# Two norms between mixer and channel mixer, taken by halves of the tokens

## The chip, the core and the metric

The kernel runs on one core of a Trainium2 chip. TensorE (PE) multiplies matrices into PSUM, VectorE (DVE) and ScalarE (ACT) do the elementwise work, GpSimd (POOL) a few small powers, and SyncE (SP) issues the DMAs. The metric is the device time of one execution in microseconds (us), lower is better.

## The reference

A hybrid layer (dilated attention and a linear recurrence) is followed by two layers of a second block. Only this block is touched. Each layer adds four token mixers, projected by `w_out`, to the residual stream `x` (512 tokens of 1024 channels), norms the sum, and adds a channel mixer:

```
x = x + mod_x[2] * token_mixers(...)          # concatenate([y_a, y_b, y_c, y_d]) @ w_out
x = x + mod_x[5] * channel_mixer(modulate(rms_norm_2(x, norm2_g[l]), mod_x[3], mod_x[4]), w1, w2)

rms_norm_2(x, g) = x * rsqrt(mean(x * x, axis=-1) + EPS) * g
modulate(h, shift, scale) = h * (1 + scale) + shift
channel_mixer(h, w1, w2) = square(relu(h @ w1)) @ w2      # 1024 -> 4096 -> 1024
```

In layer 0 a second stream of 256 context tokens goes through the same channel mixer. The norm needs the whole sum of a token's 1024 channels, so nothing of the channel mixer can start for a token before the last mixer's projection of that token is done.

## The kernel before

Activations lie transposed: 8 tiles of 128 channels by 512 tokens (context: 8 of 128 by 256). Every matrix product is made of three float32r matmuls (`mm3`, L157 to L159: high weights by high activations, high by low, low by high), so each operand is kept as a high part (ACT: `whi` L149, `h` L711) and a low part (DVE: `wlo` L150, `h` L712). Three buffers each hold the high and the low halves of a weight block (`W_BUFS = 3`), so a cast of new weights waits until PE has read the block three before.

The engines run their own queues in order; the order comes from a list scheduler with priorities. `tc.high_priority(offset=n)` moves instructions forward, and `bg(n)` (a negative offset) back.

At the place in question, once in each of the two layers, PE finishes the attention of the last mixer ("b"). `out_part("b")` then multiplies its result `y` by `w_out`: 8 output tiles of 128x512, 6 matmuls each. DVE adds every tile to the residual `x` (L1139), ACT squares it (L217), DVE adds the squares into `acc` (L221). Behind the last tile, `rstd_bcast` sums `acc` and the last square over channels on PE with one-column matmuls (L208, the squares are the weights, a column of ones moves), DVE scales (L233), POOL takes the power (L225), DVE spreads the result (L238), and PE transposes it into all partitions (L241). `modulate` then makes each of the 8 tiles of `h`: DVE multiplies (L709), ACT makes the high part (L711), DVE the low part (L712). The first pair of up-projection tiles (`up(0)`, called block 0 below; `up(1)` is block 1) goes through `gemm` with `together=True`, so that its tiles advance side by side. ACT takes the relu (L1283), DVE squares it (L1284) and splits the result into `hid`.

Of the kernel before, what the change touches and what calls it, by code (L numbers as in the profile page):

```python
# [10 lines left out]
F32 = mybir.dt.float32  # L11
# [8 lines left out]
P = 128  # L20
NT = 8
# [58 lines left out]
def tile_net(ctx: ExitStack, tc: tile.TileContext, wst, vec, crow, lrow, sgw, cst, xT, xN, cT, out):  # L80
# [117 lines left out]
    class Sums:  # L198


        def __init__(self, n, acc=None, bank=None):
            self.n, self.acc, self.bank, self.parts = n, acc, bank or (lambda: ps.mm()), [] if acc is None else [acc]

        def finish(self):
            pt, nt = self.bank(), self.n // P
            for k, a in enumerate(self.parts):
                for i in range(nt):
                    T.matmul(pt[:, i:i + 1], a[:, i * P:(i + 1) * P], ones1, start=k == 0 and i == 0,  # L208
                             stop=k == len(self.parts) - 1 and i == nt - 1, skip_group_check=True)
# [15 lines left out]
        G.tensor_tensor(rs[:, :n], ms, neghalf[:, :n], ALU.pow)  # L225
        return rs

    def rstd_bcast(pool, sums, n, inv, tile=None):
# [10 lines left out]
        pb = bank()  # L239
        for i in range(nt):  # L240
            T.transpose(pb[:, i * P:(i + 1) * P], rb[:, i], ident)  # L241
        return pb[:, :n]


    def silu_row(pool, tmp, name, idx):

        raw = pool.tile([P, 1024], F32, tag=name, name=name)
        nc.sync.dma_start(raw, crow[:, idx * 1024:(idx + 1) * 1024])
        for q in range(2):
            c = raw[:, q * 512:(q + 1) * 512]  # L250
            th = tmp("th")
            A.activation(th, c, AF.Tanh, scale=0.5)
            V.scalar_tensor_tensor(c, th, 1.0, c, op0=ALU.add, op1=ALU.mult)
        return raw
# [446 lines left out]
        else:  # L701
            affine1 = affine

    def modulate(pool, s, pb, off, acts, bufs=3):

        a_col, b_col = s.mod[:, off + 8:off + 16], s.mod[:, off:off + 8]
        for m in range(NT):
            t = pool.tile([P, s.n], F32, tag=f"r{s.name}", name=nm("mod"), bufs=bufs)
            V.scalar_tensor_tensor(t, s.x[m], a_col[:, m:m + 1], pb, op0=ALU.mult, op1=ALU.mult)  # L709
            a, b = acts[m], b_col[:, m:m + 1]  # L710
# [18 lines left out]
    def xsums():  # L729
        return Sums(SX, xp.tile([P, SX], F32, tag="acc", name=nm("acc")))  # L730
# [77 lines left out]
    class Mixer:  # L808
# [325 lines left out]
                    heads_norm(po, r1)  # L1134


        def add(self, m, p, done):
            s = self.s
            V.scalar_tensor_tensor(s.x[m], p, s.mod[:, 16 + m:17 + m], s.x[m], op0=ALU.mult, op1=ALU.add)  # L1139
            if done:  # L1140
                done(m)

        def out_part(self, names, done=None, bank=None):

# [44 lines left out]
    for l in range(2):  # L1189
# [60 lines left out]


        full = [sx, sc] if l == 0 else [sx]
        g_n, mlp = open_pool("mlp")
        sx.h = [mlp.tile([P, 2, SX], F32R, tag="hx", name=nm("h"), bufs=8) for _ in range(NT)]
        if l == 0:
            sc.h = [mlp.tile([P, 2, SC], F32R, tag="hc", name=nm("h"), bufs=8) for _ in range(NT)]
            g_c, cp = open_pool("cp", side="right")
            load_ctx(cp, lambda m: c_dram[m], cp)
            pbc = rstd_bcast(mlp, sc.acc, SC, 1.0 / 1024)
        modulate(mlp, sx, pbx, 24, sx.h)  # L1260
        if l == 0:
            modulate(mlp, sc, pbc, 24, sc.h)
            g_r, rowp = open_pool("rows1", side="right")
            rawa_bufs[0] = 1
            junk_fn[0] = lambda n: mlp.tile([P, SX], F32, tag="rx", name=nm(n), bufs=3)
            c2 = silu_row(rowp, junk_fn[0], "c2row", 1)
            cc = silu_row(rowp, junk_fn[0], "ccrow", 2)
            steps = ada_steps(1, lambda n="j": junk_fn[0](n))
        hid = {}
        nhid = [0]  # L1270

# [8 lines left out]
        def up(b):  # L1280
            def evac(s, i, p):
                r = mlp.tile([P, s.n], F32, tag=f"r{s.name}", name=nm("r"), bufs=3)
                A.activation(r, p, AF.Relu)  # L1283
                V.scalar_tensor_tensor(r, p, 0.0, r, op0=ALU.max, op1=ALU.mult)  # L1284
                a = hid_tile(s)
                split(a, r)
                hid[(s.name, 2 * b + i)] = a

            gemm(wblock((f"up{l}", b), 4, 256), 4, [(s, s.n, s.h) for s in full], evac, together=b == 0)

        def down(c, strs, last):
            if last:
# [11 lines left out]
                if l == 0:  # L1304
                    pump(1)

        for b in range(4):
            up(b)
        for c in range(4):
            if c < 3:  # L1310
                up(4 * c + 4)
                down(c, full, False)
                for b in range(4 * c + 5, 4 * c + 8):
                    up(b)
                    if l == 0:
                        pump(1)
            else:
                down(c, [sx], True)
                pbx = rstd_bcast(mlp, sx.acc, SX, 1.0 / 1024)
                if l == 0:  # L1320
                    pump(24)
                    for t, q in affine1:
                        ada_affine(t, vc("ada_b1"), q)
                    sx.mod = modx[1]
                    sx.h = [xact("h") for _ in range(NT)]
                    modulate(mlp, sx, pbx, 0, sx.h)
                    down(c, [sc], True)
                    close_pool(g_r)
# [32 lines left out]
VP = 7000  # L1361
HPS = 400
PT_BUFS = 2
PSA = dict(g=3, mm=2, po=1, big=1)
PSD = dict(g=3, mm=1, po=1, sc3=1)

# [138 lines left out]
```

## Time and profile before

| | |
|---|---|
| three timed runs, us | 2176.32, 2177.66, 2178.42 |
| median, us | 2177.66 |
| the profiled execution: its time, us | 2175.18 |
| the profiled execution: its span, first to last instruction, us | 2173.3 |
| mean granted TensorE clock | 0.978 |

The span lies inside the execution; 1.9 us of its time lie around it. [...]

### The profile page before, as it was taken

To read this page: it belongs to the slowest core of one execution; us is meant where nothing else is said; L and a number is where in the kernel's file an instruction comes from. 1 tells how busy PE (TensorE), PEld (TensorE's weight loads), DVE (VectorE), ACT (ScalarE), POOL (GpSimd) and SP (SyncE) were. 2 spreads that over 40 slices of the span, in tenths; PEclk is the share of its full clock that TensorE was granted. 3 is DMA by queue.
4 is the path that set the end of the run, shared out by engine and by line. 5 is a ranking of instruction groups with operands and counts; after the bars stand their busy time and mean duration, and the time that the engine had idled before them with its cause. 6 is when DMAs were issued, how large, how long until landed. Compare 5 with 4: busy or idle time off the path is not lost.

```text
span 2173.3 us, 28000 instructions
## 1 busy us (share of the span) xinstructions
PE 2053.4 (94%) x11020; PEld 1758.3 (81%) x11020; DVE 1424.4 (66%) x2351; ACT 810.1 (37%) x1266; POOL 27.4 (1%) x28
## 2 busy tenths in 40 slices
PE   7989999999999988998999999999998998999997
PEld 5778788778889777876888888888887787888886
DVE  8778999843458999778354645534798766443444
ACT  3565333432344533645312313123434544232331
POOL 0000000000000000000000000000000000000000
PEclk9999999999999999998999999999999998999998
DMA  8523666523335444222232454422413212333331
GB/s 314 171 92 95 197 222 204 181 94 105 109 111 168 124 121 127 78 78 79 67 127 88 138 169 150 155 67 89 135 59 107 83 59 69 97 97 97 97 97 58
DMA packets 84388, 259.47 MB, mean 119 GB/s; under 512 B 11424, under 2 KB 20256, under 8 KB 84256
## 3 DMA queue, kind: packets, MB, share of 16 engines
q1 hardware_dynamic: 84256, 257.67, 37.6%
q8 instruction: 87, 1.43, 0.3%
q14 instruction: 45, 0.37, 0.1%
HBM read 242.95 MB, written 5.24 MB: 114 GB/s over the span
## 4 chain that ended last, share of the span: by engine, by line
PE 72%; DVE 18%; DMA 3%; issue 3%; ACT 3%; POOL 1%; SPq 0%; POOLq 0%; DVEq 0%; ACTq 0%
PE mm L157 15%; PE mm L159 15%; PE mm L158 15%; PE g L157 5%; PE g L158 5%; PE g L159 5%; DVE wlo L150 3%; DVE ya L872 2%; PE po L1084 2%; DVE rawa L263 2%; DVE j L263 1%; PE sc L1057 1%; DMA rawa<-wst 1%; PE mm L1081 1%; PE mm L208 1%
## 5 line engine op out<-in xcount | busy, mean ns | idle before, releaser
L149 ACT CAST whi<-raw 128x1024 fp32r<-128x1024 f32 x312 | 326.9, 1050 | 536.7 <-PE mm L158 387.4
L150 DVE TENSOR_TENSOR wlo<-raw,whi 128x1024 fp32r<-128x1024 f32 x312 | 380.5, 1222 | 210.7 <-ACT whi L149 205.9
L157 PE MATMUL mm<-h,whi 128*128 128x512 f32 (+1 forms) x992 | 361.0, 366 | 5.7 <-ACT h L338 3.6
L158 PE MATMUL mm<-h,whi 128*128 128x512 f32 (+1 forms) x992 | 361.7, 365 | 0.9 <-DVE h L712 0.9
L159 PE MATMUL mm<-h,wlo 128*128 128x512 f32 (+1 forms) x992 | 361.1, 364 | 0.8 <-DVE wlo L150 0.8
L159 PE MATMUL mm<-hid,wlo 128*128 128x512 f32 (+1 forms) x768 | 272.6, 355 | 1.0 <-DVE wlo L150 1.0
L157 PE MATMUL mm<-hid,whi 128*128 128x512 f32 (+1 forms) x768 | 273.0, 355 | 0.0
L158 PE MATMUL mm<-hid,whi 128*128 128x512 f32 (+1 forms) x768 | 272.8, 355 | 0.0
L157 PEld LDWEIGHTS mm<-h,whi 128*128 128x128 f32 x992 | 188.8, 191 | 37.1 <-ACT h L338 4.0
L158 PEld LDWEIGHTS mm<-h,whi 128*128 128x128 f32 x992 | 188.7, 190 | 31.5 <-DVE h L712 1.9
L157 PE MATMUL g<-h,whi 128*128 128x512 f32 x512 | 205.7, 402 | 8.6 <-DVE v L508 6.0
L159 PEld LDWEIGHTS mm<-h,wlo 128*128 128x128 f32 x992 | 188.6, 190 | 31.2 <-DVE wlo L150 2.0
L158 PE MATMUL g<-h,whi 128*128 128x512 f32 x512 | 204.8, 400 | 0.0
L159 PE MATMUL g<-h,wlo 128*128 128x512 f32 x512 | 204.3, 399 | 0.3 <-DVE wlo L150 0.3
L159 PEld LDWEIGHTS mm<-hid,wlo 128*128 128x128 f32 x768 | 146.1, 190 | 21.5 <-DVE wlo L150 1.4
L157 PEld LDWEIGHTS mm<-hid,whi 128*128 128x128 f32 x768 | 146.4, 191 | 20.2
L158 PEld LDWEIGHTS mm<-hid,whi 128*128 128x128 f32 x768 | 146.3, 191 | 20.0
L1284 DVE SCALAR_TENSOR_TENSOR r<-mm,r 128x512 f32<-128x512 f32 x96 | 57.4, 599 | 114.1 <-ACT r L1283 114.0
L157 PEld LDWEIGHTS g<-h,whi 128*128 128x128 f32 x512 | 98.4, 192 | 26.9 <-issue 6.2
L159 PEld LDWEIGHTS g<-h,wlo 128*128 128x128 f32 x512 | 98.1, 192 | 19.3 <-DVE wlo L150 0.7
L158 PEld LDWEIGHTS g<-h,whi 128*128 128x128 f32 x512 | 98.3, 192 | 17.9
L872 DVE SCALAR_TENSOR_TENSOR ya<-glu,caw,ya 128x512 f32<-128x512 f32 (+1 forms) x180 | 111.6, 656 | 0.5
(309 smaller groups left out, 3462.7 us busy)
## 6 DMA issues: line engine op xcount, KB each, us to landing
raw<-wst SPq DMA_DIRECT2D x312, 512.0 KB, 3.9
rawa<-wst SPq DMA_DIRECT2D x120, 512.0 KB, 4.6
qst<-q SPq DMA_DIRECT2D x48, 64.0 KB, 2.0
kst<-k SPq DMA_DIRECT2D x48, 64.0 KB, 2.0
kst<-k SPq DMA_DIRECT2D x72, 32.0 KB, 2.1
x<-xT SPq DMA_DIRECT2D x4, 512.0 KB, 5.0
hs_d<-c SPq DMA_DIRECT2D x4, 512.0 KB, 2.6
hq<-hs_d SPq DMA_DIRECT2D x4, 512.0 KB, 5.5
```

Of the source, the lines that this page charges most:

```text
L149: A.copy(hi, src)
L150: V.tensor_sub(lo, src, hi.bitcast(F32))
L157: T.matmul(ps, lh, rh, start=start, stop=False)
L158: T.matmul(ps, lh, rl, start=False, stop=False)
L159: T.matmul(ps, ll, rh, start=False, stop=stop)
L208: T.matmul(pt[:, i:i + 1], a[:, i * P:(i + 1) * P], ones1, start=k == 0 and i == 0, stop=k == len(self.parts) - 1 and i == nt - 1, skip_gr ...
L263: V.tensor_tensor_reduce(o, w, row, 0.5, 0.0, ALU.mult, ALU.add, d)
L872: V.scalar_tensor_tensor(self.ya[m], x, w, self.ya[m], op0=ALU.mult, op1=ALU.add)
L1057: T.matmul(st[:, o:e], hd.q[:, w, qt * P:(qt + 1) * P], hd.k[:, w, o - w * nkeys:e - w * nkeys], start=True, stop=True, skip_group_check=True)
L1081: T.transpose(pt[:, i * P:(i + 1) * P], pw[0][:, t0 + i * P:t0 + (i + 1) * P], ident)
L1084: T.matmul(hd.po[:, qt, h % 2], pth[:, i * P:(i + 1) * P], ss.v[:, kt, h], start=i == 0 and qt == 0 and h % 2 == 0, stop=i == nk - 1 and q ...
L1284: V.scalar_tensor_tensor(r, p, 0.0, r, op0=ALU.max, op1=ALU.mult)
```

## The change

`out_tokens` replaces `out_part("b")`: it makes the 8 output tiles for tokens 0 to 255, then for tokens 256 to 511, in matmuls of 256 columns. The sums no longer go through `acc`: right behind each add, ACT squares the 128x256 half tile, and PE multiplies its two 128-token pieces by ones into a PSUM bank of the half (`Sums(now=...)`, `nb`), moved back by 10 or 60 in the scheduler's priority. Each half has its own `rstd_bcast`, its own `modulate` into its half of the tiles `h`, and its own pass of `up(0)`. `gemm` with `together=True` now goes over channels outside and tiles inside. In layer 0 the context's norm, modulation and first up-projection pair are written ahead of the first half's, at a priority raised by 150. PSUM is shared out as 6 banks and 2 for the halves, where it was 8.

```diff
             for h, (hi, lo) in enumerate(halves):
-                for (mi, (key, n, acts)), p in zip(grp, pss_):
-                    c = slice(mi * P, (mi + 1) * P)
-                    for k in range(kn):
+                for k in range(kn):
+                    for (mi, (key, n, acts)), p in zip(grp, pss_):
+                        c = slice(mi * P, (mi + 1) * P)
                         kk = h * kn + k
                         a = acts[kk]
                         mm3(p[:, :n], hi[:, k, c], lo[:, k, c], a[:, 0], a[:, 1], kk == 0, kk == kt - 1)
...
+        def product(self, pt, a, first, last):
+            for i in range(self.n // P):
+                T.matmul(pt[:, i:i + 1], a[:, i * P:(i + 1) * P], ones1, start=first and i == 0,
+                         stop=last and i == self.n // P - 1, skip_group_check=True)
...
             A.activation(sq, src, AF.Square)
-            if self.acc is None or m == NT - 1:
+            if self.now is not None:
+                with bg(self.back if m >= 6 else 10):
+                    self.product(self.now[:, SC:], sq, m == 0, m == NT - 1)
+            elif self.acc is None or m == NT - 1:
                 self.parts.append(sq)
...
+        def out_tokens(self, n, w, sl, done):
+
+            for m in range(NT):
+                p = ps.mm()[:, :SC]
+                hi, lo = w[m // 4]
+                c = slice(m % 4 * P, (m % 4 + 1) * P)
+                for kk in range(2):
+                    a = self.y[n, kk][:, :, sl]
+                    mm3(p, hi[:, kk, c], lo[:, kk, c], a[:, 0], a[:, 1], kk == 0, kk == 1)
+                self.add(m, p, done, sl)
...
-        ps = PS("ps_e", mm=8)
-        sx.acc = xsums()
-        mx.out_part("b", lambda m: sx.acc.add(None, sx.x[m], m, mx.tt("sq")))
-        pbx = rstd_bcast(mix, sx.acc, SX, 1.0 / 1024, tile=mx.tt("rb"))
+        ps = PS("ps_e", mm=6, nb=2)
+        g_n, nrm = open_pool("nrm", side="right")
+        wb = [whalf((f"out{l}", 2 + h), 1, 512) for h in range(2)]
+        pbs = []
+        for t in range(2):
+            acc, sl = Sums(SC, now=ps.mm("nb"), back=SUM_BACK[t]), TOK[t]
+            mx.out_tokens("b", wb, sl, lambda m: acc.add(
+                None, sx.x[m][:, sl], m, nrm.tile([P, SC], F32, tag="sq", name=nm("sq"), bufs=4)))
+            pbs.append(rstd_bcast(None, acc, SC, 1.0 / 1024, back=RB_BACK[t],
+                                  tile=nrm.tile([P, SC], F32, tag="rb", name=nm("rb"), bufs=2)))
+        close_pool(g_n)
...
+            with tc.high_priority(offset=CTX_HP):
+                load_ctx(cp, lambda m: c_dram[m], cp)
+                pbc = rstd_bcast(mlp, sc.acc, SC, 1.0 / 1024)
+                modulate(mlp, sc, pbc, 24, sc.h)
+        modulate(mlp, sx, pbs[0], 24, sx.h, sl=TOK[0])
+        up0 = wblock((f"up{l}", 0), 4, 256)
+        if l == 0:
+            up(0, up0, [sc])
+        up(0, up0, [sx], TOK[0])
+        modulate(mlp, sx, pbs[1], 24, sx.h, sl=TOK[1])
+        up(0, up0, [sx], TOK[1])
```

Three places show what this does to the engines' order, all in layer 0; layer 1 has the first two in the same form.

On PE, in the projection of the last mixer (`mm` are output tiles, `nb_8630` is the first half's bank of sums, `sq_8639` and `sq_8651` are squares of its first and second tile), before and then now:

```order
L157 MATMUL mm_8643<-y_8319,whi_8616 128x512
L158 MATMUL mm_8643<-y_8319,whi_8616 128x512
L159 MATMUL mm_8643<-y_8319,wlo_8617 128x512
L157 MATMUL mm_8643<-y_8606,whi_8616 128x512
L158 MATMUL mm_8643<-y_8606,whi_8616 128x512
L159 MATMUL mm_8643<-y_8606,wlo_8617 128x512
```

```order
L157 MATMUL mm_8655<-y_8606,whi_8618 128x256
L158 MATMUL mm_8655<-y_8606,whi_8618 128x256
L207 MATMUL nb_8630<-ones_66,sq_8639 128x1 x2
L159 MATMUL mm_8655<-y_8606,wlo_8619 128x256
L157 MATMUL mm_8667<-y_8319,whi_8618 128x256
L158 MATMUL mm_8667<-y_8319,whi_8618 128x256
L159 MATMUL mm_8667<-y_8319,wlo_8619 128x256
L207 MATMUL nb_8630<-ones_66,sq_8651 128x1
L157 MATMUL mm_8667<-y_8606,whi_8618 128x256
L207 MATMUL nb_8630<-ones_66,sq_8651 128x1
```

The sums of a half tile now stand among the projection's matmuls, the first of them 17 matmuls behind its start; of the 16 half tiles of a layer, 8 have their two columns together and 8 have a matmul in between, and those of the last three half tiles stand behind the projection.

On ACT, at the end of the projection (`whi_9030` and `whi_9229` are the weights of block 1's first half; their buffer is that of the second half of `w_out`), before and then now:

```order
L217 ACTIVATE sq_8690<-x_4800 128x512
L149 CAST whi_9030<-raw_9032 128x1024
L217 ACTIVATE sq_8701<-x_4801 128x512
L217 ACTIVATE sq_8712<-x_4802 128x512
L711 ACTIVATE h_8740<-mod_8811,der 128x512
```

```order
L223 ACTIVATE sq_8804<-x_4800 128x256
L149 CAST whi_9229<-raw_9231 128x1024
L223 ACTIVATE sq_8816<-x_4801 128x256
L223 ACTIVATE sq_8828<-x_4802 128x256
L723 ACTIVATE h_8855<-mod_8918,der 128x256
```

The cast that waits for PE's last read of `w_out` stays ahead of the last two squares.

On DVE, behind the last add of layer 0 (`nb_8735` is the second half's bank, `mm_8904` the context's sums, `h_8855` the context's first tile), now:

```order
L1152 SCALAR_TENSOR_TENSOR x_4802<-mm_8820,der,x_4802 128x256
L150 TENSOR_TENSOR wlo_9230<-raw_9231,whi_9229 128x1024
L242 TENSOR_SCALAR ms_8833<-nb_8735 128x2
L242 TENSOR_SCALAR ms_8909<-mm_8904 128x2
L247 COPY rb_8832<-rs_8835 128x256
L247 COPY rb_8913<-rs_8911 128x256
L721 SCALAR_TENSOR_TENSOR mod_8918<-xc_8867,der,mm_8915 128x256
L721 SCALAR_TENSOR_TENSOR mod_8922<-xc_8870,der,mm_8915 128x256
L721 SCALAR_TENSOR_TENSOR mod_8926<-xc_8875,der,mm_8915 128x256
L724 SCALAR_TENSOR_TENSOR h_8855<-mod_8918,der,h_8855 128x256
```

The context's modulation, which is now the first work behind the norm, stands behind the statistics of the second half; behind it come the first half's 8 tiles, and the second half's follow behind the first half's relu work.

## Rows read from the trace of the kernel before

**Rows 1.** Page, part 1: busy us, share of the span, instructions.

```profile
PE 2053.4 (94%) x11020; PEld 1758.3 (81%) x11020; DVE 1424.4 (66%) x2351; ACT 810.1 (37%) x1266; POOL 27.4 (1%) x28
```

**Rows 2.** PE's waits, 1017 to 1300: who, us, times, longest.

```profile
PE mm L159 <- DVE wlo L150: 1.0, 1, 1.0
```

**Rows 3.** PE's timeline, layer 0: start, us, engine, line, [idle before].

```profile
982.43 0.40 PE L157 MATMUL mm<-y,whi 128*128 128x512 f32 x1
...
993.41 0.40 PE L159 MATMUL mm<-y,wlo 128*128 128x512 f32 x1
997.41 1.56 PE L208 MATMUL mm<-ones,acc 128*128 128x1 f32 x8 [3.60 <-DVE acc L221]
...
1006.91 0.78 PE L157 MATMUL mm<-h,whi 128*128 128x512 f32 x1
...
1044.92 0.40 PE L157 MATMUL mm<-h,whi 128*128 128x512 f32 x1
```

**Rows 4.** PE's timeline, layer 1.

```profile
1784.86 0.40 PE L157 MATMUL mm<-y,whi 128*128 128x512 f32 x1
...
1795.83 0.40 PE L159 MATMUL mm<-y,wlo 128*128 128x512 f32 x1
1799.83 1.83 PE L208 MATMUL mm<-ones,acc 128*128 128x1 f32 x8 [3.60 <-DVE acc L221]
...
1807.94 2.07 PE L157 MATMUL mm<-h,whi 128*128 128x512 f32 x4 [1.60 <-ACT h L711]
...
1832.46 0.39 PE L157 MATMUL mm<-h,whi 128*128 128x512 f32 x1
```

**Rows 5.** Windows, layer 0: us, busy (count) of each engine, PEclk, DMA.

```profile
993.80:1006.90 13.10, 6.21 (x31) 6.04 (x31) 6.16 (x12) 3.39 (x5) 1.70 (x2) 0.65 0.47 161
1006.90:1011.20 4.30, 4.01 (x11) 2.72 (x10) 4.30 (x8) 2.04 (x3) 0.00 (x0) 0.50 0.00 0
```

**Rows 6.** PE's timeline where two conv tiles' sums stand among matmuls.

```profile
1717.93 0.95 PE L208 MATMUL g<-ones,sq 128*128 128x1 f32 x8
1718.73 0.48 PE L159 MATMUL g<-h,wlo 128*128 128x512 f32 x1
1719.05 0.39 PE L157 MATMUL g<-h,whi 128*128 128x512 f32 x1
```

**Rows 7.** PE's timeline in the up-projection: 24 rows lie between each two.

```profile
1201.77 0.28 PE L157 MATMUL mm<-h,whi 128*128 128x256 f32 x1
...
1204.64 0.40 PE L157 MATMUL mm<-h,whi 128*128 128x512 f32 x1
...
1210.11 0.28 PE L157 MATMUL mm<-h,whi 128*128 128x256 f32 x1
```

**Rows 8.** DVE's timeline: adds, modulation and low weights.

```profile
985.31 2.29 DVE L1139 SCALAR_TENSOR_TENSOR x<-mm,der,x 128x512 f32<-128x512 f32 x3
...
994.73 1.23 DVE L150 TENSOR_TENSOR wlo<-raw,whi 128x1024 fp32r<-128x1024 f32 x1
...
1007.75 2.06 DVE L709 SCALAR_TENSOR_TENSOR mod<-x,der,mm 128x512 f32<-128x512 f32 x3
...
1015.68 1.26 DVE L709 SCALAR_TENSOR_TENSOR mod<-xc,der,mm 128x256 f32<-128x256 f32 x3
1016.86 1.29 DVE L712 SCALAR_TENSOR_TENSOR h<-mod,der,h 128x256 fp32r<-128x256 f32 x3
...
1787.49 1.40 DVE L1139 SCALAR_TENSOR_TENSOR x<-mm,der,x 128x512 f32<-128x512 f32 x2
```

**Rows 9.** ACT's timeline, end of layer 0's projection and context.

```profile
993.65 1.04 ACT L149 CAST whi<-raw 128x1024 fp32r<-128x1024 f32 x1 [0.33 <-PE mm L158]
...
1016.33 1.29 ACT L711 ACTIVATE h<-mod,der 128x256 fp32r<-128x256 f32 x3
```

**Rows 10.** POOL's timeline, context's power.

```profile
1005.49 0.70 POOL L225 TENSOR_TENSOR rs<-ms,neghalf 128x2 f32<-128x2 f32 x1 [3.46 <-DVE ms L233]
```

**Rows 11.** Windows, attention of layer 1.

```profile
1730.00:1735.00 5.00, 2.51 (x16) 1.87 (x16) 3.71 (x6) 1.88 (x4) 0.00 (x0) 1.00 0.26 75
```

More of the change, by code (lines that the diff above doesn't have):

```diff
@@ L198, in tile_net, with __init__ @@
     class Sums:
-        def __init__(self, n, acc=None, bank=None):
+        def __init__(self, n, acc=None, bank=None, now=None, back=0):
             self.n, self.acc, self.bank, self.parts = n, acc, bank or (lambda: ps.mm()), [] if acc is None else [acc]
+            self.now, self.back = now, back
+        def product(self, pt, a, first, last):
+            for i in range(self.n // P):
+                T.matmul(pt[:, i:i + 1], a[:, i * P:(i + 1) * P], ones1, start=first and i == 0,
+                         stop=last and i == self.n // P - 1, skip_group_check=True)
         def finish(self):
-            pt, nt = self.bank(), self.n // P
+            if self.now is not None:
+                return self.now[:, SC:]
+            pt = self.bank()
             for k, a in enumerate(self.parts):
-                for i in range(nt):
-                    T.matmul(pt[:, i:i + 1], a[:, i * P:(i + 1) * P], ones1, start=k == 0 and i == 0,
-                             stop=k == len(self.parts) - 1 and i == nt - 1, skip_group_check=True)
+                self.product(pt, a, k == 0, k == len(self.parts) - 1)
             return pt
@@ L217, in add @@
             A.activation(sq, src, AF.Square)
-            if self.acc is None or m == NT - 1:
+            if self.now is not None:
+                with bg(self.back if m >= 6 else 10):
+                    self.product(self.now[:, SC:], sq, m == 0, m == NT - 1)
+            elif self.acc is None or m == NT - 1:
                 self.parts.append(sq)
@@ L226, in rstd_small, with rstd_bcast @@
         return rs
-    def rstd_bcast(pool, sums, n, inv, tile=None):
+    def rstd_bcast(pool, sums, n, inv, tile=None, back=0):
         nt = n // P
@@ L238, in rstd_bcast @@
         V.tensor_copy(rb, rs[:, :nt].unsqueeze(2).broadcast_to([P, nt, P]))
-        pb = bank()
-        for i in range(nt):
-            T.transpose(pb[:, i * P:(i + 1) * P], rb[:, i], ident)
+        pb = bank() if sums.now is None else sums.now
+        with bg(back):
+            for i in range(nt):
+                T.transpose(pb[:, i * P:(i + 1) * P], rb[:, i], ident)
         return pb[:, :n]
@@ L1134, in attention, with add @@
                     heads_norm(po, r1)
-        def add(self, m, p, done):
+        def add(self, m, p, done, sl=slice(None)):
             s = self.s
-            V.scalar_tensor_tensor(s.x[m], p, s.mod[:, 16 + m:17 + m], s.x[m], op0=ALU.mult, op1=ALU.add)
+            x = s.x[m][:, sl]
+            V.scalar_tensor_tensor(x, p, s.mod[:, 16 + m:17 + m], x, op0=ALU.mult, op1=ALU.add)
             if done:
                 done(m)
+        def out_tokens(self, n, w, sl, done):
[7 more added lines that the diff above has]
+                self.add(m, p, done, sl)
         def out_part(self, names, done=None, bank=None):
@@ L1252, in tile_net @@
         full = [sx, sc] if l == 0 else [sx]
[L1253 to L1268, printed above, removed]
         hid = {}
@@ L1278, in hid_tile, with up, up_block @@
             return mlp.tile([P, 2, SX], F32R, tag="hidx", name=nm("hid"), bufs=2)
-        def up(b):
+        def up(b, w, strs, sl=None):
             def evac(s, i, p):
-                r = mlp.tile([P, s.n], F32, tag=f"r{s.name}", name=nm("r"), bufs=3)
+                n, tag = (s.n, f"r{s.name}") if sl is None else (SC, "rc")
+                r = mlp.tile([P, n], F32, tag=tag, name=nm("r"), bufs=3)
                 A.activation(r, p, AF.Relu)
                 V.scalar_tensor_tensor(r, p, 0.0, r, op0=ALU.max, op1=ALU.mult)
[L1285 to L1289, printed above, removed]
+                j = (s.name, 2 * b + i)
+                if j not in hid:
+                    hid[j] = hid_tile(s)
+                split(hid[j][:, :, sl or slice(0, n)], r)
+            gemm(w, 4, [(s, s.n, s.h) if sl is None else (s, SC, [h[:, :, sl] for h in s.h]) for s in strs],
+                 evac, together=sl is not None or strs == [sc])
+        g_n, mlp = open_pool("mlp")
+        sx.h = [mlp.tile([P, 2, SX], F32R, tag="hx", name=nm("h"), bufs=8) for _ in range(NT)]
+        if l == 0:
+            sc.h = [mlp.tile([P, 2, SC], F32R, tag="hc", name=nm("h"), bufs=8) for _ in range(NT)]
+            g_c, cp = open_pool("cp", side="right")
+            with tc.high_priority(offset=CTX_HP):
[4 more added lines that the diff above has]
+        up0 = wblock((f"up{l}", 0), 4, 256)
+        if l == 0:
+            up(0, up0, [sc])
+        up(0, up0, [sx], TOK[0])
+        modulate(mlp, sx, pbs[1], 24, sx.h, sl=TOK[1])
+        up(0, up0, [sx], TOK[1])
+        if l == 0:
+            g_r, rowp = open_pool("rows1", side="right")
+            rawa_bufs[0] = 1
+            junk_fn[0] = lambda n: mlp.tile([P, SX], F32, tag="rx", name=nm(n), bufs=3)
+            c2 = silu_row(rowp, junk_fn[0], "c2row", 1)
+            cc = silu_row(rowp, junk_fn[0], "ccrow", 2)
+            steps = ada_steps(1, lambda n="j": junk_fn[0](n))
+        def up_block(b):
+            up(b, wblock((f"up{l}", b), 4, 256), full)
         def down(c, strs, last):
@@ L1305, in down @@
                     pump(1)
-        for b in range(4):
-            up(b)
+        for b in range(1, 4):
+            up_block(b)
         for c in range(4):
             if c < 3:
-                up(4 * c + 4)
+                up_block(4 * c + 4)
                 down(c, full, False)
                 for b in range(4 * c + 5, 4 * c + 8):
-                    up(b)
+                    up_block(b)
                     if l == 0:
@@ L1363 @@
 PT_BUFS = 2
+TOK = [slice(0, 256), slice(256, 512)]
+RB_BACK = [60, 240]
+SUM_BACK = [10, 60]
+CTX_HP = 150
 PSA = dict(g=3, mm=2, po=1, big=1)
```

10 lines of the change are left out of this document (6 added, 4 removed).

## The prediction

> **What bounds the kernel now.** The page's first part comes first: PE is busy for 94% of the span, the next engine for 66% [rows 1]. PE's waits in the channel mixer of layer 0 are a single one of 1.0 us [rows 2], so a microsecond gained or lost at the seam ahead of it is carried to the end. The seam is then read from PE's timeline. In layer 0 the projection runs from 982.43, its last matmul starts at 993.41, and the first up-projection matmul starts at 1006.91: PE does little for 13 us but 3.60 us of waiting for `acc` and the norm's chain [rows 3]. In layer 1 the same stretch lasts from 1795.83 to 1807.94 [rows 4]. [...] The reader should look for two totals that I use as marks: from the projection's start to the first matmul of block 2, 62.5 us in layer 0 (982.43 to 1044.92) and 47.6 us in layer 1 (1784.86 to 1832.46) [rows 3, 4].
>
> **What one piece costs.** Between the marks in the up-projection, 24 matmuls of 256 columns take 2.87 us and 24 of 512 take 5.47 [rows 7]: 0.120 and 0.228 each, so halving costs 0.012 a matmul. The projection's 48 took 0.233 each [rows 3]. On DVE three 256-column operations take 1.26 to 1.29 us where three of 512 take 2.06; with the overlap of ends, 0.40 against 0.66 each [rows 8]. ACT's take 0.43 [rows 9].
>
> The sums of squares are the dear part. Their closest rows are 8 rows (four 128-token columns, two passes each, for float32) among other matmuls at full clock: from their start to the next matmul 0.80 us, and that matmul's successor follows after 0.32 where 0.23 is usual [rows 6]. So a pass is 0.10 us and the return to the other matmuls 0.09. A half tile has four passes: 0.49 us; where a matmul stands between its columns, the return is paid twice: 0.58. Before, these passes ran while PE had nothing else to do [rows 3, 4]; now 13 of the 16 half tiles of a layer stand inside the projection. Bounds: 0.12 if all the passes' loads hid behind a matmul of 256 columns, 0.98 if everything ran at half clock. I take 0.49 and 0.58, the rows being the same instruction in the same surroundings.
>
> **Layer 0, step by step, from 982.43.**
> - The projection's matmuls: 96 x 0.120 = 11.5 us (11.2 before).
> - A new wait. The first sum stands 17 matmuls in, so PE arrives at 984.5. DVE's first add starts only at 985.31, behind the casts of weights, which don't move [rows 8]; with 0.48 for it and 0.43 for ACT's square PE goes on at 986.3: 1.8 us. Everything behind on PE waits with it, since its matmuls keep their order.
> - Sums: five half tiles at 0.49 and eight at 0.58: 7.1 us.
> - The context's sums (8 rows, 0.89) and the first half's two transposes (0.5 by the same prices): 1.4 us.
>
> The projection so ends at 982.43 + 11.5 + 1.8 + 7.1 + 1.4 = 1004.2, where it ended at 993.6. The tail behind it stays: ACT's cast waits for PE's last read of `w_out` and is still ahead of the last two squares, 1.04 us [rows 9]; then two squares (0.8), the sums (0.5), DVE's scaling (0.2), POOL twice in a row (1.4) [rows 10], DVE's copy (0.3), transposes (0.5), one multiplication (0.48) and ACT's high part (0.43), with some 0.1 at each of nine hand-overs: 6.6 us. The first up-projection matmul starts at 1010.8, 3.9 us later than before.
>
> From there DVE sets the pace: a tile needs 2 x 0.40 = 0.80 us of it, and gives PE 6 x 0.120 = 0.72 us of work. The context's 8 tiles and the first half's 8 take 12.8 us from the first multiplication at 1009.8, so PE is through both at about 1023.6 with its last group and the part spent at half clock. Then, new: PE stands until relu, two squarings, the first multiplication of the second half and two casts are through, 0.4 to 0.5 us each: 3.1 us. The second half's 8 tiles take 6.4 us, the low weights ahead of the last two 1.1 [rows 8], the last group 0.7: block 0 is done at about 1034.9. By then 2.8 us of block 1's 16.7 (48 x 0.228 + 48 x 0.120) are done among the waits, as the order on PE shows; 13.9 remain. Block 2 begins at 1048.8, against 1044.92: **+4 us**, and with the clock uncertain in the new tail, which is as thin as the old one, I put +4.5.
>
> **Layer 1, from 1784.86**, has no context: 11.5 + 7.1 + 0.5, and a wait of 1.5, since DVE's first add starts at 1787.49 [rows 8] and PE arrives at 1786.9. The projection ends at 1805.5. The cast, two squares and the last three sums last until 1808.0, and the first up-projection matmul starts there, as before (1807.94); the first half's norm is ready by then. DVE again needs 0.80 a tile, plus low weights, a scaling and a copy (1.6): PE ends the first half near 1816, waits 1.2 for the first tile of the second, and ends that near 1826.2 (6.4 for tiles, 1.6 for relu work and 1.1 for weights). 14 matmuls of block 1 (3.2 us) are done by then, 7.7 of its 10.9 us remain: block 2 begins near 1834 instead of 1832.46, **+1.5 to +2**.
>
> **The sum** is +6.5 us. Put as work: sums, halving and transposes add 10 us a layer to PE, while its idle and half-clock time falls from 18 to about 11 us in layer 0 and from 14 to about 6 in layer 1. Against the profiled execution's own 2175.18 us (1.9 of it outside the span) this is 2181.7; that execution lies 2.5 below the runs' median, so for a median I give 2177.66 + 6.5 = **2184**. Memory, DMA order and everything outside the two seams keep their order, and no DMA is added, so those I cost at nothing; weights are cast at the same places relative to PE.
>
> [...] The rows say that a halved DVE operation costs 0.40 where a whole one costs 0.66, so a split tile pays 0.14 more [rows 8]. [...]
>
> **Rivals.**
> - *The sums cost PE little* (chance 0.10). If their loads run beneath the neighbours' matmuls, at 0.12 a half tile, the 26 inside the two projections cost 3 us instead of 14: 2173. Against it: in the rows the loads lengthen the stream by 0.88 us for eight. The point that decides faster or slower than before is 0.30 us a half tile, 6.5 us being shared by 26.
> - *The halves close the gaps as they are laid out to* (0.05): if DVE keeps ahead of PE, the idle time of both seams falls to about 2 us each, and 2167 results. [...] Here 0.80 against 0.72 us a tile speaks against it: at this place DVE is saturated.
> - *The gains and losses nearly cancel* (0.20): a shorter wait for the first square, a full clock at layer 0's seam and a shorter tail are worth 1 to 2 us each; two or three of them give 2178 to 2182.
> - *The clock falls inside the projection* (0.07), where PE's work is now thin: if two thirds of it run at 0.50, both layers lose about 9 us more, 2202. Against it: in the attention a window with PE busy for 2.51 of 5 us kept the full clock [rows 11], and the projection stays far busier.
>
> The forecast itself, 2182 to 2192, has 0.58. The range that leaves out the second and the last rival is 2173 to 2193; it takes in the low end of the sums' price. Within 0.2%, 4.4 us, is what a measurement of this kernel can't tell from no change. Slower than that: forecast and clock, and a little less for the forecast's lower edge, 0.66; same: 0.22; faster: 0.12.
>
> **What would show it.** Right: the projection of layer 0 lasts about 22 us on PE, with a wait for a square near its start of 1.5 to 2 us; sums of a half tile cost 0.4 to 0.6 us; the up-projection of layer 0 starts near 1011 and that of layer 1 near 1808; PE waits some 3 us for the second half's first tile in layer 0. Wrong, if the sums come nearly free, if block 2 of layer 0 begins before 1045, or if the granted clock is 0.50 inside the projection.

## The result, and the profile after

The changed kernel takes 2201.28 us (median of 4 runs, 2193.60 to 2203.24) against 2176.99 for the kernel before (4 runs, 2174.94 to 2178.42): 1.0108 times as long, 95% interval 1.009 to 1.0126. Slower was forecast, but by 6.5 us and not by 24, and the range ended at 2193.

The profiled execution took 2201.78 us, its span is 2199.7. The page's first part of the changed kernel, the row that answers to [rows 1]:

```profile
PE 2089.7 (95%) x11308; PEld 1802.9 (82%) x11308; DVE 1426.5 (65%) x2399; ACT 817.3 (37%) x1306; POOL 29.1 (1%) x30
```

PE is busier by 36 us than before, more than the 26.4 by which the span grew: the time wasn't lost to idling, PE's own work takes longer. Its timeline at layer 0's seam in the changed kernel (as in [rows 3]) shows where:

```profile
979.71 0.28 PE L157 MATMUL mm<-y,whi 128*128 128x256 f32 x1
...
983.58 0.61 PE L207 MATMUL nb<-ones,sq 128*128 128x1 f32 x4 [1.66 <-ACT sq L223]
...
986.89 0.42 PE L207 MATMUL nb<-ones,sq 128*128 128x1 f32 x2
...
989.02 0.42 PE L207 MATMUL nb<-ones,sq 128*128 128x1 f32 x2
...
1012.77 0.56 PE L159 MATMUL mm<-y,wlo 128*128 128x256 f32 x1
...
1020.11 0.80 PE L157 MATMUL mm<-h,whi 128*128 128x256 f32 x2 [1.11 <-ACT h L723]
...
1036.65 0.85 PE L157 MATMUL mm<-h,whi 128*128 128x256 f32 x4 [2.36 <-ACT h L723]
...
1059.23 0.40 PE L157 MATMUL mm<-h,whi 128*128 128x512 f32 x1
```

The first matmul is the projection's start, the last row block 2's. The wait for the first square is there (1.66 us). Behind it the projection's last matmul starts 33.06 us after the first, where it was 10.98 before [rows 3]. From one tile's sum to the next 2.13 us pass (986.89 to 989.02). The windows of layer 0 in the changed kernel (columns as in [rows 5]) show the reason:

```profile
975.00:980.00 5.00, 5.00 (x25) 4.11 (x24) 4.12 (x9) 3.67 (x10) 0.00 (x0) 1.00 0.00 0
980.00:985.00 5.00, 3.34 (x26) 3.13 (x26) 3.95 (x6) 1.73 (x4) 0.00 (x0) 0.94 0.48 131
985.00:990.00 5.00, 5.00 (x25) 5.00 (x25) 0.97 (x2) 1.21 (x3) 0.00 (x0) 0.50 0.25 82
...
1005.00:1010.00 5.00, 5.00 (x26) 5.00 (x25) 2.05 (x4) 0.83 (x2) 0.00 (x0) 0.50 0.29 79
...
1025.00:1030.00 5.00, 5.00 (x42) 5.00 (x42) 5.00 (x14) 2.86 (x8) 0.00 (x0) 0.96 0.00 0
```

The granted clock falls about a microsecond behind the wait (1.00 in 983 to 984, 0.70 in 984 to 985) and is 0.50 of full speed from then to 1025, in every window left out here too. Through the projection PE reads busy for 5.00 of 5 us all the same. Layer 1 repeats it; its timeline and one window:

```profile
1798.38 0.28 PE L157 MATMUL mm<-y,whi 128*128 128x256 f32 x1
...
1802.03 0.61 PE L207 MATMUL nb<-ones,sq 128*128 128x1 f32 x4 [1.44 <-ACT sq L223]
...
1828.89 0.56 PE L159 MATMUL mm<-y,wlo 128*128 128x256 f32 x1
...
1832.20 0.78 PE L157 MATMUL mm<-h,whi 128*128 128x256 f32 x2
...
1891.51 0.39 PE L157 MATMUL mm<-hid,whi 128*128 128x512 f32 x1
```

```profile
1805.00:1810.00 5.00, 5.00 (x25) 5.00 (x25) 0.97 (x2) 1.08 (x3) 0.00 (x0) 0.50 0.03 8
```

The timeline's last row is the first matmul of the down-projection. I use it as the end mark from here on, since it is a single clear row in both layers; in layer 0 it gives the same as block 2's start to 0.1 us. Before, it stood at

```profile
1094.96 0.40 PE L157 MATMUL mm<-hid,whi 128*128 128x512 f32 x1
...
1865.10 0.39 PE L157 MATMUL mm<-hid,whi 128*128 128x512 f32 x1
```

and in the changed kernel at 1109.27 in layer 0. From the projection's start that is 112.53 and 80.24 us before, and 129.56 and 93.13 now: +17.0 and +12.9.

### The profile page after: what moved, and what is told of

It is laid out like the page before. It is cut to its first block, busy times and chain, and to the rows that moved or that the text cites. A ratio compares the mean times of both kernels' runs of the same rounds, so it can differ in the third digit from the quotient of the medians.

```text
span 2199.7 us, 28684 instructions
## 1 busy us (share of the span) xinstructions
PE 2089.7 (95%) x11308; PEld 1802.9 (82%) x11308; DVE 1426.5 (65%) x2399; ACT 817.3 (37%) x1306; POOL 29.1 (1%) x30
## 3 DMA queue, kind: packets, MB, share of 16 engines
q8 instruction: 89, 1.46, 0.3%
## 4 chain that ended last, share of the span: by engine, by line
PE 75%; DVE 16%; DMA 3%; issue 2%; ACT 2%; POOL 1%; SPq 1%; POOLq 0%; DVEq 0%; ACTq 0%
PE mm L157 16%; PE mm L158 16%; PE mm L159 16%; PE g L157 5%; PE g L159 5%; PE g L158 5%; DVE wlo L150 3%; DVE ya L884 2%; PE po L1096 2%; DVE rawa L273 2%; DMA rawa<-wst 1%; PE sc L1069 1%; PE mm L1093 1%; DVE j L273 1%; PE g L164 1%
## 5 line engine op out<-in xcount | busy, mean ns | idle before, releaser
L149 ACT CAST whi<-raw 128x1024 fp32r<-128x1024 f32 x312 | 327.0, 1050 | 545.0 <-PE mm L158 393.2
L157 PE MATMUL mm<-h,whi 128*128 128x512 f32 (+1 forms) x1024 | 363.1, 360 | 7.9 <-ACT h L723 4.3
L159 PE MATMUL mm<-h,wlo 128*128 128x512 f32 (+1 forms) x1024 | 366.5, 359 | 0.9 <-DVE wlo L150 0.9
L158 PE MATMUL mm<-h,whi 128*128 128x512 f32 (+1 forms) x1024 | 367.3, 360 | 0.0
L157 PEld LDWEIGHTS mm<-h,whi 128*128 128x128 f32 x1024 | 193.9, 192 | 37.2 <-ACT h L723 5.3
L159 PEld LDWEIGHTS mm<-h,wlo 128*128 128x128 f32 x1024 | 195.8, 191 | 30.1 <-DVE wlo L150 2.2
L158 PEld LDWEIGHTS mm<-h,whi 128*128 128x128 f32 x1024 | 196.0, 191 | 28.6 <-DVE h L724 0.3
L1301 DVE SCALAR_TENSOR_TENSOR r<-mm,r 128x512 f32<-128x512 f32 (+1 forms) x100 | 58.0, 582 | 112.9 <-ACT r L1300 112.5
```

The source lines that it names most:

```text
L149: A.copy(hi, src)
L157: T.matmul(ps, lh, rh, start=start, stop=False)
L158: T.matmul(ps, lh, rl, start=False, stop=False)
L159: T.matmul(ps, ll, rh, start=False, stop=stop)
```

## The experiments

All runs but e3_dense, which is described below, by layer 0 / layer 1, in us. The first three columns come from the one traced execution of each kernel, the last is the median of all its runs. "Wait" is PE's wait for the first square, "projection" runs from its first matmul's start to its last one's, "to the down-projection" from the same start to the mark above.

| kernel | wait | projection | to the down-projection | median, and that of before beside it |
|---|---|---|---|---|
| before | none | 10.98 / 10.97 | 112.53 / 80.24 | 2176.99 |
| the change | 1.66 / 1.44 | 33.06 / 30.51 | 129.56 / 93.13 | 2201.28, 2176.99 |
| e1_later | 0.58 / 0.38 | 18.58 / 17.48 | 113.69 / 79.30 | 2175.06, 2175.14 |
| e8_between | 1.07 / 0.86 | 19.38 / 18.28 | 115.49 / 79.85 | 2177.24, 2174.93 |
| e5_nowait | none | 18.17 / 17.28 | 114.27 / 79.13 | 2174.17, 2174.93 |
| e2_acc | none | 16.27 / 13.64 | 114.65 / 78.83 | 2174.83, 2175.14 |
| e4_whole | 0.89 / 0.65 | 17.43 / 17.16 | 114.82 / 81.97 | 2178.18, 2175.14 |
| e9_waitonly | 1.65 / 1.46 | 19.88 / 18.79 | 118.51 / 82.92 | 2183.97, 2175.82 |
| e6_onepass | 1.70 / 1.49 | 18.88 / 17.76 | 115.32 / 79.46 | 2174.51, 2174.93 |
| e10_mixed | 1.68 / 1.48 | 26.70 / 25.58 | 123.16 / 87.42 | 2187.65, 2175.82 |
| e7_later_onepass | 0.64 / 0.43 | 15.73 / 14.70 | 111.32 / 76.35 | 2171.09, 2174.93 |
| e11_best | 0.63 / 0.42 | 14.84 / 14.63 | 111.38 / 76.11 | 2170.10, 2175.78 |

At the start there were three suspects for the fall of the clock: the one-column sums among the matmuls (my theory), the wait ahead of them, and the halved matmuls. The first four kernels were chosen so that each suspect gives its own pattern.

**e1_later.** The first sum stands later, the rest stays among the matmuls. In the traces 26 matmuls start ahead of the first sum here, against 17 in the changed kernel; 22 do in e8_between, 13 in e5_nowait and 17 in e9_waitonly, two fewer each time than the expectations say.

```diff
-                with bg(self.back if m >= 6 else 10):
+                with bg(self.back if m >= 6 else 26):
```

> Only the priority of the sums of the first six tiles of each half changes (moved back by 26 instead of 10): the first sum stands 11 matmuls later in the projection, so PE should hardly wait for the first square, and the other sums stay among the projection's matmuls. If the one-column sums among the 256-column matmuls make the clock fall (my theory): granted clock 0.50 for most of the projection in both layers, projection about 30 us, 2195 to 2202 us. If the wait of 1.4 to 1.7 us for the first square makes it fall and the sums only follow: clock 1.00 through the projection, about 20 us for it, 2180 to 2187 us. If the halved matmuls alone make it fall: 0.50, 2195 to 2202.

PE's timeline and one window, layer 0:

```profile
983.25 0.38 PE L207 MATMUL nb<-ones,sq 128*128 128x1 f32 x2 [0.58 <-ACT sq L223]
...
984.50 0.28 PE L207 MATMUL nb<-ones,sq 128*128 128x1 f32 x2
...
985.66 0.28 PE L207 MATMUL nb<-ones,sq 128*128 128x1 f32 x2
...
1004.48 0.80 PE L157 MATMUL mm<-h,whi 128*128 128x256 f32 x2 [1.11 <-ACT h L723]
```

```profile
985.00:990.00 5.00, 5.00 (x46) 5.00 (x45) 1.93 (x4) 2.01 (x5) 0.00 (x0) 1.00 0.15 60
```

The clock stays at 1.00 through both projections with nearly the same sums, and the whole loss is gone: ratio to before 0.9993 (0.9977 to 1.001). My theory falls. The rows also give the sums' price at full clock: 1.16 us from tile to tile (984.50 to 985.66), less 6 x 0.120, is 0.44.

**e2_acc.** DVE adds up the squares of a half, PE sums twice at its end.

```diff
-                with bg(self.back if m >= 6 else 10):
-                    self.product(self.now[:, SC:], sq, m == 0, m == NT - 1)
+                if m == 0:
+                    self.hold = sq
+                elif m < NT - 1:
+                    V.tensor_add(self.hold, self.hold, sq)
+                else:
+                    with bg(self.back):
+                        self.product(self.now[:, SC:], self.hold, True, False)
+                        self.product(self.now[:, SC:], sq, False, True)
```

> The halves stay, but DVE adds up the squares of a half as it did before, and PE multiplies by ones only twice for each half, behind its matmuls. If the one-column sums make the clock fall, or the wait for the first square: clock 1.00 through the projection, which then goes at DVE's pace (16 half tiles at 0.48 for the add of x and 0.40 for the add of squares, about 14 us, and some 3 us ahead of the first), 2172 to 2180 us. If the halved matmuls alone make the clock fall: 0.50 in the projection, 2188 to 2200.

2174.83 us, ratio 0.9999 (0.9982 to 1.0015). The halved matmuls alone don't hold the clock down; the projection goes at DVE's pace, and PE waits 3.3 us at its end. In layer 0 the clock dips for a moment (0.79 in 995 to 1000) behind a wait of 1.11 us and the first half's two sums, and is back by 1005 under plain matmuls (0.21 us apart up to 1001.1, 0.12 behind).

**e3_dense.** Each half tile's sum is one dense matmul, with the wait kept; POOL's power goes over 256 columns.

```diff
-                    self.product(self.now[:, SC:], sq, m == 0, m == NT - 1)
+                    T.matmul(self.now[:, :SC], onesr, sq, start=m == 0, stop=m == NT - 1)
...
+            V.tensor_scalar(ms, acc.now[:, :SC], 1.0, EPS, op0=ALU.mult, op1=ALU.add)
+            G.tensor_tensor(rb, ms, neghalf[:, :1].broadcast_to([P, SC]), ALU.pow)
```

> The halves and the place of the sums stay, but each half tile's sum is one dense float32r matmul of 256 columns: the square (now written as float32r) moves and a 128x128 matrix of 1/1024 stands as the weights, so the mean square comes out in all partitions; DVE adds the constant, POOL takes the power on 128x256, no transposes. The wait for the first square stays. If the one-column sums make the clock fall: clock 1.00 in the projection, which takes 11.5 + 1.9 + 1.5 = 15 us, 2172 to 2184 us (POOL's power on 256 columns is not known). If the wait makes it fall: 0.50 behind the wait, about 2190. If halved matmuls do: the same.

As a time it failed: 2312.66 us, since POOL's power took 41.2 us for 256 columns, four times (a group of its operations by line):

```profile
L1280 POOL TENSOR_TENSOR rb<-ms,neghalf 128x256 f32<-128x256 f32 x4 | 164.7, 41167 | 44.8 <-DVE ms L1278 44.8
```

But the stretch ahead of that answers the question. Its timeline and windows, layer 0:

```profile
990.87 0.38 PE L228 MATMUL nb<-sq,onesr 128*128 128x256 f32 x1 [1.66 <-ACT sq L225]
```

```profile
990.00:995.00 5.00, 4.13 (x33) 4.05 (x33) 2.75 (x7) 2.47 (x6) 0.00 (x0) 1.00 0.56 188
995.00:1000.00 5.00, 5.00 (x41) 4.81 (x40) 3.19 (x7) 2.55 (x6) 2.27 (x1) 1.00 0.01 2
```

The same wait, 1.66 us, and no fall; nor in layer 1 (1.45 us, and 1.00 from 1850 to 1860). So such a wait doesn't always bring a fall.

**e4_whole.** The kernel before with 512 columns, and only the sums put among the matmuls.

```diff
-            if self.acc is None or m == NT - 1:
+            if self.now is not None:
+                with bg(10):
+                    for i in range(4):
+                        T.matmul(self.now[:, i:i + 1], sq[:, i * P:(i + 1) * P], ones1, ...)
+            elif self.acc is None or m == NT - 1:
```

> The kernel before (512 columns, one norm) with only the sums changed: no adding up of squares on DVE, the four one-column float32 products of each tile stand among the projection's matmuls, no wait near its start. If the one-column sums make the clock fall: 0.50 in the projection of both layers, which takes some 28 us, 2195 to 2205 us. If the wait or the halved matmuls make it fall: clock 1.00, projection about 18 us, 2176 to 2183.

1.00 to the projection's end, 2178.18 us, ratio 1.001 (0.9992 to 1.0028): with a wait of 0.89 and 0.65 us, against the theory of the sums once more.

**e5_nowait, e8_between.** Two ways to vary the wait under nearly the same stream: squares of the old `x` for five tiles of the first half, and a first sum moved back by 20.

```diff
+            if early and m < 5:
+                done(m)
             V.scalar_tensor_tensor(x, p, s.mod[:, 16 + m:17 + m], x, op0=ALU.mult, op1=ALU.add)
-            if done:
+            if done and not (early and m < 5):
                 done(m)
```

> The changed kernel with its order on PE nearly untouched (the first sum 15 matmuls behind the projection's start, the sums one-column float32 as before), but in the first half the squares of tiles 0 to 4 are taken from x ahead of the add, so PE needn't wait for them; this changes what is computed (these five squares are those of the old x). If the wait of 1.4 to 1.7 us, followed by thin sums, made the clock fall: clock 1.00 through the projection, which takes 17 to 19 us, and 2172 to 2180 us. If the place of the sums in the order made the difference between the changed kernel and the one with later sums, and not the wait: 0.50 in the projection, 2195 to 2202 us.

```diff
-                with bg(self.back if m >= 6 else 10):
+                with bg(self.back if m >= 6 else 20):
```

> As the kernel with later sums, but moved back by 20 instead of 26: the first sum stands 24 matmuls in (17 in the changed kernel, 28 there), so PE should wait some 0.8 to 1.1 us in layer 0 and 0.6 to 0.9 in layer 1, between the two kernels. If the length of the wait ahead of the thin stretch decides: the clock holds in layer 1 at least, and the time is 2175 to 2190; if any wait there lets it fall: 2193 to 2201.

Windows of layer 0 in e5_nowait, then the wait and a window in e8_between:

```profile
985.00:990.00 5.00, 5.00 (x45) 5.00 (x44) 2.27 (x5) 0.92 (x3) 0.00 (x0) 1.00 0.34 111
990.00:995.00 5.00, 5.00 (x44) 5.00 (x44) 2.39 (x6) 2.65 (x6) 0.70 (x1) 1.00 0.00 0
```

```profile
984.98 0.38 PE L207 MATMUL nb<-ones,sq 128*128 128x1 f32 x2 [1.07 <-ACT sq L223]
```

```profile
985.00:990.00 5.00, 5.00 (x43) 5.00 (x44) 2.19 (x5) 1.96 (x5) 0.00 (x0) 1.00 0.39 118
```

Both keep 1.00 through both projections (18.17 and 17.28 us; 19.38 and 18.28): 2174.17 us, 0.9991 (0.9978 to 1.0004), and 2177.24 us, 1.0009 (0.9996 to 1.0023). The first one keeps nearly the changed kernel's order, with the same two-pass sums at the same spacing, and loses the wait, so the wait is needed for the loss.

**e6_onepass.** The wait stays, the sums are single passes.

```diff
-                    self.product(self.now[:, SC:], sq, m == 0, m == NT - 1)
+                    for i in range(2):
+                        T.matmul(self.now[:, SC + 2 * i:SC + 2 * i + 2], sq[:, i * P:(i + 1) * P], ones1r, ...)
```

> The changed kernel with its wait for the first square, its sums as one-column products of squares written as float32r, a single pass each instead of two (two equal columns of ones, of which one is used). If any sums of one or two columns behind the wait make the clock fall: 0.50 in the projection, 2190 to 2197 us. If the thin stretch behind the wait has to be as long as with two passes (0.44 us a half tile there, some 0.25 here): clock 1.00, projection about 16 us, 2170 to 2178.

Neither came true as written: the clock fell, and came back by itself. The time, 2174.51 us (0.999, 0.9978 to 1.0002), lies in the second range, but not for its reason. Windows, layer 0:

```profile
985.00:990.00 5.00, 3.78 (x21) 3.78 (x22) 2.19 (x6) 1.64 (x4) 0.00 (x0) 0.72 0.53 197
990.00:995.00 5.00, 5.00 (x42) 4.97 (x40) 2.47 (x6) 2.01 (x5) 0.08 (x1) 0.94 0.00 2
995.00:1000.00 5.00, 5.00 (x46) 4.99 (x44) 3.80 (x8) 2.59 (x6) 0.61 (x1) 1.00 0.00 0
```

So there are two questions, what makes it fall and what keeps it down. The next two kernels take them apart.

**e9_waitonly, e10_mixed.** In the first, only one sum stands behind the wait, and 46 plain matmuls follow; in the second, the first half has two-pass sums and the second half single-pass ones.

```diff
-                with bg(self.back if m >= 6 else 10):
+                with bg(10 if m == 0 else self.back if m >= 6 else 75):
```

> The changed kernel with the wait and the first sum where they are (first sum 19 matmuls in), but the sums of the half's other tiles moved back by 75, so that 46 matmuls of 256 columns follow the first sum with nothing between them; the sums of both halves then stand in the second half. If the wait makes the clock fall and the thin sums only keep it from coming back: 0.50 for a few us behind the wait, 1.00 again before the second half, 2173 to 2182 us. If it takes wait and thin sums together for it to fall: 1.00 throughout, 2172 to 2178. If any fall lasts to the projection's end: 2190 to 2200.

```diff
+                    if self.back == SUM_BACK[0]:
                         self.product(self.now[:, SC:], sq, m == 0, m == NT - 1)
+                    else:
+                        for i in range(2):
+                            T.matmul(self.now[:, SC + 2 * i:SC + 2 * i + 2], sq[:, i * P:(i + 1) * P], ones1r, ...)
```

> The changed kernel with its wait and its two-pass sums in the first half, but single-pass sums (float32r squares) in the second half. If the two-pass sums keep the clock down and single-pass ones let it come back: 0.50 from behind the wait through the first half, 1.00 again some us into the second half, between the changed kernel and the one with single-pass sums everywhere, 2182 to 2191 us. If the clock, once down, stays down to the projection's end whatever the sums are: 0.50 to the end, 2193 to 2200.

Windows of layer 0, first e9_waitonly, then e10_mixed (its first single-pass sum stands at 1002.89):

```profile
985.00:990.00 5.00, 5.00 (x31) 5.00 (x31) 2.05 (x5) 1.62 (x4) 0.00 (x0) 0.66 0.32 106
990.00:995.00 5.00, 5.00 (x44) 4.85 (x42) 2.73 (x6) 2.67 (x7) 0.00 (x0) 1.00 0.01 2
```

```profile
990.00:995.00 5.00, 5.00 (x26) 5.00 (x25) 1.14 (x3) 1.25 (x3) 0.00 (x0) 0.50 0.01 6
...
1000.00:1005.00 5.00, 5.00 (x25) 5.00 (x25) 1.81 (x5) 1.12 (x3) 0.70 (x1) 0.50 0.00 0
1005.00:1010.00 5.00, 5.00 (x44) 5.00 (x44) 2.89 (x5) 2.36 (x6) 0.00 (x0) 1.00 0.15 27
```

With plain matmuls behind the first sum the clock is back by 990; with two-pass sums it stays at 0.50 through the whole half, and comes back under single-pass sums. In layer 1 of e10_mixed, where the first single-pass sum stands at 1815.73, it came back later (0.50 in 1815 to 1820, 0.92 in the next window). The times are 2183.97 (1.0026, 1.0008 to 1.0043), 2 us above the first range, and 2187.65 us (1.0051, 1.003 to 1.0072), inside its first range. The runs of both scatter, and the traces show one end of each: e9_waitonly's traced execution took 2179.15 us (its runs 2178.70 to 2187.45), e10_mixed's 2195.19, its slowest (from 2183.29). What lifts e9_waitonly's median above the range therefore isn't in its trace. What the trace does show is a dearer second half: the sums of both halves stand there, and the first up-projection matmul comes 28.38 us after the start, against 25.10 in e1_later.

**e7_later_onepass, e11_best.** The later first sum together with single-pass sums; then also, in layer 0, the context behind the first half instead of ahead of it. The first has the edits of e1_later and e6_onepass:

```diff
+                with bg(self.back if m >= 6 else 26):
+                    for i in range(2):
+                        T.matmul(self.now[:, SC + 2 * i:SC + 2 * i + 2], sq[:, i * P:(i + 1) * P], ones1r, ...)
```

> The kernel with later sums (first sum 28 matmuls in) and the single-pass sums together. Clock 1.00 in the projection by every theory left. If a pass costs what it did (0.10 us and the return), 13 half tiles a layer save some 0.2 us each, 2.6 us a layer on the way to block 2: 2168 to 2173 us where the kernel before has 2175. If the passes are not what the sums cost: the same as with later sums alone, 2173 to 2177.

The second adds to it:

```diff
-                pbc = rstd_bcast(mlp, sc.acc, SC, 1.0 / 1024)
-                modulate(mlp, sc, pbc, 24, sc.h)
         modulate(mlp, sx, pbs[0], 24, sx.h, sl=TOK[0])
         up0 = wblock((f"up{l}", 0), 4, 256)
+        up(0, up0, [sx], TOK[0])
         if l == 0:
+            pbc = rstd_bcast(mlp, sc.acc, SC, 1.0 / 1024)
+            modulate(mlp, sc, pbc, 24, sc.h)
             up(0, up0, [sc])
-        up(0, up0, [sx], TOK[0])
```

> The kernel with later single-pass sums, and in layer 0 the context's norm, modulation and first up-projection pair written behind the first half's instead of ahead of them. There the first half's norm has been ready since the middle of the projection (as in layer 1, where the first up-projection matmul starts 2.3 us behind the projection's last matmul against 6.5 in layer 0), so PE should start some 4 us earlier in layer 0, with a shorter time at 0.50; the context then stands between the halves. If the tail of layer 0 was a loss on the way to the end: block 2 of layer 0 some 3 to 4 us earlier, 2166 to 2169 us. If DVE's pace or the waits between the three parts take it back: 2170 to 2173, as before this edit.

e7_later_onepass takes 2171.09 us, 0.9974 times the kernel before (0.9961 to 0.9987): a version that beats both, the kernel before by 3.8 us (0.26%, with an interval clear of 1). The projection is 2.85 and 2.78 us shorter than in e1_later, as the passes' price foretold. e11_best, 2170.10 us and 0.9978 (0.9966 to 0.999), adds nothing that can be measured, although its first up-projection matmul starts 17.22 us behind the projection's start instead of 22.22. PE's waits from 1000 to 1050, first in e7_later_onepass and then in e11_best:

```profile
PE mm L159 <- ACT h L727: 3.5, 2, 2.4
PE nb L255 <- DVE rb L251: 1.4, 1, 1.4
PE nb L229 <- ACT sq L225: 0.9, 1, 0.9
```

```profile
PE mm L159 <- ACT h L727: 2.9, 3, 1.7
PE nb L229 <- ACT sq L225: 0.9, 1, 0.9
```

The waits shrink by 2.0 us only, and the clock falls a second time, behind the new wait of 1.7 us (0.66 in 1015 to 1020, where e7_later_onepass kept 1.00). The first fall is shorter by as much, so each kernel spends some 10 us at 0.50 there (by the mean clock from 1000 to 1045, 0.89 in both). The end mark is where it was, 111.38 against 111.32. Where else the 5 us go, DVE's pace above all, wasn't tried.

## Why the prediction was wrong

**The step that failed** is the clock inside the projection, which the sum puts at nothing: it prices layer 0's projection at full clock, 21.8 us, and 33.1 were measured. The prediction names the fall as its last rival, "the clock falls inside the projection", with two thirds of it at 0.50, 9 us more in each layer, and 2202 us: the measured time is 2201.28. It got 0.07, on the argument that a window of the attention with PE busy for 2.51 of 5 us kept the full clock [rows 11] and that the projection stays far busier. The busy share was the wrong thing to compare. In the changed kernel PE is busy for 5.00 of 5 us at 0.50; the page counts one-column matmuls as busy time like any others (0.42 us for two).

That the rival's 2202 and the measured 2201.28 agree so closely is partly luck. Between the marks the two layers lost 17.0 and 12.9 us, 29.9 in all, where the rival makes 24.5 of it; but the traced execution started layer 0's projection 2.7 us earlier than the one before the change and took 0.8 us less from the mark there to layer 1's, so that its span grew by 26.4.

**What the runs put in its place.** Two things together: PE's wait for the first square, behind which the clock fell, and the two-pass sums, under which it stayed down.
- The fall: with a wait of 1.44 to 1.70 us and a thin first sum the clock fell in all eight seams measured (the change, e6_onepass, e9_waitonly, e10_mixed). With no wait or waits of up to 1.07 us behind the first 13 to 26 matmuls it held in all six of e1_later, e5_nowait and e8_between. The runs without traces fit: none of the 30 of these three took more than 2183.13 us, none of the changed kernel's four less than 2193.60. In e2_acc a wait of 1.11 us was followed by a fall (0.79 in 995 to 1000).
- The staying down: two-pass sums, 0.85 us a half tile at half clock, kept it at 0.50 to the projection's end. Under single-pass sums or plain matmuls it came back by itself: 0.94 in 990 to 995 in e6_onepass, 1.00 there in e9_waitonly, 1.00 in 1005 to 1010 in e10_mixed.
- The price in layer 0: some 80 matmuls at 0.2135 us instead of 0.120 are 7.5 us, 13 sums at 0.85 instead of about 0.5 are 4.5, 12.0 together. The projection came out 11.3 us longer than forecast (33.1 to 21.8).

Whether the first sum has to be thin for the fall isn't shown. With the long wait and dense sums the clock held in both seams of e3_dense. But PE also waits 2.1 to 2.6 us for the second half's first tile in layer 0, with only dense matmuls behind; there it fell for some 3.4 us in e6_onepass, e8_between and e9_waitonly (matmuls of 256 columns 0.21 us apart instead of 0.12), and held in the change, e1_later, e2_acc, e5_nowait, e7_later_onepass and e10_mixed. In e11_best it fell behind 1.7 us, with dense matmuls behind as well. The wait and the windows in e8_between, then in e1_later:

```profile
1022.47 0.85 PE L157 MATMUL mm<-h,whi 128*128 128x256 f32 x4 [2.35 <-ACT h L723]
```

```profile
1020.00:1025.00 5.00, 2.65 (x15) 2.29 (x14) 4.81 (x14) 3.53 (x9) 0.00 (x0) 0.87 0.02 5
1025.00:1030.00 5.00, 5.00 (x33) 4.81 (x33) 3.13 (x8) 2.46 (x5) 0.00 (x0) 0.79 0.00 0
```

```profile
1020.47 0.85 PE L157 MATMUL mm<-h,whi 128*128 128x256 f32 x4 [2.36 <-ACT h L723]
```

```profile
1020.00:1025.00 5.00, 4.53 (x34) 4.34 (x35) 5.00 (x14) 2.71 (x7) 0.00 (x0) 1.00 0.01 3
1025.00:1030.00 5.00, 5.00 (x35) 4.59 (x34) 4.47 (x9) 2.78 (x5) 0.00 (x0) 1.00 0.29 92
```

So the length of a wait doesn't settle by itself whether the clock falls behind it; what else does stays open.

**The other steps**, against the changed kernel and, at full clock, e8_between, whose wait is nearest:
- The wait for the first square: forecast 1.8 and 1.5 us, measured 1.66 and 1.44. Right, but its price was put at its own length.
- A half tile's sum: forecast 0.49 and 0.58, measured 0.44 at full clock (e1_later). Its upper bound, 0.98 "if everything ran at half clock", was close to the 0.85 that came true; but the same case slows the matmuls too, and that was not carried into the range.
- The tail of layer 0: forecast 6.6 us, measured 7.3 in the changed kernel, with the granted clock at 0.50 (before, it averaged 0.65 in the gap [rows 5]), and 6.5 in e1_later. Right.
- From the first up-projection matmul to block 2 in layer 0: forecast 38.0, measured 39.1. DVE's pace was near. The waits for the second half's first tile were 2.36 and 0.87, forecast 3.1 and 1.2.
- The whole at full clock: e8_between is 3.0 us later to the mark in layer 0 and 0.4 earlier in layer 1; with the rest of the wait (0.6 each) that makes +3.6 and +0.2 where +4.5 and +1.75 stood. By these marks the sum without the clock was too high by 2 to 3 us. Its sign isn't shown: e8_between's time can't be told from that of before (1.0009, 0.9996 to 1.0023).
- What was to show the forecast wrong, "if the granted clock is 0.50 inside the projection", is what the profile showed.

## What to carry to other kernels

Before work is put into the places between matmuls, ask what the stream looks like to the clock, not whether PE reads busy: a stream with one-column matmuls in it read as fully busy and still ran at a granted clock of 0.50 for 28 us here, to the end of layer 0's projection. A wait of a microsecond and a half on PE can cost nine times its length (1.66 us in layer 0, 15.3 us to the mark against e5_nowait) if the clock falls behind it and the stream that follows leaves it there; here nine more plain matmuls between a producer and the first instruction that waits for it (e1_later), or sums in one pass (e6_onepass), took the whole loss away. And a forecast whose rival prices a fall of the clock at three times everything else deserves its own row of evidence before it is given 7%.

## What was not expected of the hardware

- Nearly the same stream of 256-column matmuls and two-pass sums ran through a whole projection at 1.00 in e5_nowait and, once the clock had fallen, at 0.50 in the changed kernel. In these two it kept the level that it started with.
- Behind the same wait of 2.35 us, with the same dense matmuls following, the clock fell in e8_between and held in e1_later.
- A float32 power on POOL took 41.2 us for 128x256 against 0.70 for 128x2 [rows 10], about 0.16 us for each column.
- A sum of a half tile in one pass (float32r squares, two columns) costs 0.21 us at full clock, less than half of the 0.44 in two passes: in e7_later_onepass 0.93 us from tile to tile, less 6 x 0.120:

```profile
988.40 0.17 PE L229 MATMUL nb<-ones1r,sq 128*128 128x2 f32 x1
...
989.33 0.17 PE L229 MATMUL nb<-ones1r,sq 128*128 128x2 f32 x1
```
